# A hybrid attention layer: the widest level of the gated linear attention through a key-value state, and its prefix sums on VectorE

## The chip, the cores and the metric

The kernel runs on one core of a Trainium2 chip. The metric is the time of one execution on the device, in microseconds (us). Three runs of the kernel before took 887.92, 889.42 and 889.54 us; their median is 889.42 us. In this text PE is TensorE (the matmul engine), PEld its weight loads, DVE is VectorE, ACT is ScalarE, POOL is GpSimd, SP is SyncE, which here only issues transfers.

## The reference: what is computed

One decoder layer on a sequence of 512 tokens with 1024 channels, all in 32-bit floats: a layer norm, a token mixer of two branches, a residual layer norm, a squared-ReLU MLP of width 4096, and a last layer norm. One branch of the mixer is multi-head latent attention with 8 heads, the other gated linear attention (GLA) with 4 heads, keys of 128 channels and values of 256. This change is about the GLA branch alone. Cut to that branch, the reference is

```python
log_a = log_sigmoid(a_lr @ w_gla_a2 + b_gla_a2) / 16      # per token and key channel, <= 0
# b = cumsum(log_a) over tokens; for tokens i >= j:
# scores[i, j] = sum_d q[i, d] * k[j, d] * exp(b[i, d] - b[j, d])
# o[i] = sum_{j <= i} scores[i, j] * v[j]
o_gla = rms_norm(o) * silu(r)          # then a projection, gated and merged with the other branch
```

## The kernel before

Most matmuls take 32-bit data in a rounded format (fp32r), one record each in the trace. Each operand is split into a high part and a remainder: ACT copies the high part (`hi`), DVE subtracts it (`lo`), and each product is three matmuls, hi·hi, hi·lo and lo·hi. The helper `split` (L104 to L110) does this for activations, `pump` (L179, L180) for weights. Matmuls on plain 32-bit operands also occur; the profile shows two records for each of those.

The GLA scores are not computed in chunks but in levels. For s = 1, 2, 4, ... 256 the tokens are cut into blocks of s, and a level gives the scores between each right block (queries) and the left block beside it (keys). Each level needs the decays inside a block: `rp` holds two rows of 512 running sums, R (from a key to the end of its left block) and P (from the start of the right block to a query). `vec(s)` lets ACT take the exponential of them (E, L637) and DVE multiply keys and queries by it (M, L640 and L644). PE multiplies the halves of M to scores in a bank named `px` (L693, L696, L700). `take` copies them from the bank: DVE under a mask into the four diagonal 128x128 blocks SD for s up to 64, and by `split` for s = 128 (`s128`) and s = 256 (`s256`). `advance(s)` turns the sums of level s into those of 2s: two additions on POOL, each of 256 elements per partition (L619 for R, L620 for P). The next `vec` waits for both.

`gla_out(h)` multiplies the scores of a head with the values. With four blocks of 128 tokens there are ten pairs (j, i) with j up to i, each three matmuls with 256 columns, 30 for a head (L741 to L743). ACT squares each result with its sum (`osq`, L745), POOL and DVE normalise, DVE multiplies with the gate `Rg` (L755), PE transposes (L761).

The values V and the gates R are projected for a pair of heads at a time, in `proj_v(hp)` and `proj_r(hp)`. Each multiplies all 512 tokens with 512 weight columns, in four accumulator banks, one per block of 128 tokens. The evacuation splits each bank by head, 256 columns at a time: `Vh[h]` (two tiles, hi and lo, for all tokens of one head) and `Rg[h]`.

The order of the work comes from three things. The projections are the backbone: after each of a projection's eight inner steps, `tick` lets two "lanes" go one step, the levels (four heads in turn, `lane_levels`) and the outputs (`lane_out`). These lanes run beside proj_v(0), proj_r(0), proj_v(1), proj_r(1) and then the four gate projections "g" of the branch merge, between two of which stands the projection `qr` of the rotary queries. A guard in proj_v(1), `levels_upto(1)`, runs the levels of heads 0 and 1 to their end before that projection's banks are read out. Finally the framework simulates the program while it is built and puts each engine's instructions in the order that its simulation prefers; on the chip each engine takes its own in that fixed order and waits on semaphores. Accumulators have four banks named `mm`, all else shares four named `px`. Large tiles of 4 KB per partition come from a pool of 24 (tag A): V, R, the running sums, the split scores, and also the gate tiles `gt` of the "g" projections.

## Time and profile before

| What | Value |
|---|---|
| Median of three runs | 889.42 us |
| The profiled execution's own time | 889.34 us |
| Its span in the trace | 887.4 us |
| GLA levels and outputs in the trace | about 96 to 276 us |
| First matmul of the projection that reads the GLA output | about 322 us |
| Instructions in the trace | 11559 |

Times in the trace count from the start of the span. A row of a timeline has the start, the time of the group, engine, line, operation, what it writes and reads, the shape, and in brackets the idle time before it. A matmul's time in the trace is from its start to its modelled end, and the next one begins before that end; so the rate of PE is read from the distance between starts. Rows of groups have count, summed time and mean in ns.

### The profile page before, as it was taken

To read this page: it belongs to the slowest core of one execution; us is meant where nothing else is said; L and a number is where in the kernel's file an instruction comes from. 1 tells how busy PE (TensorE), PEld (TensorE's weight loads), DVE (VectorE), ACT (ScalarE), POOL (GpSimd) and SP (SyncE) were. 2 spreads that over 40 slices of the span, in tenths; PEclk is the share of its full clock that TensorE was granted. 3 is DMA by queue.
4 is the path that set the end of the run, shared out by engine and by line. 5 is a ranking of instruction groups with operands and counts; after the bars stand their busy time and mean duration, and the time that the engine had idled before them with its cause. 6 is when DMAs were issued, how large, how long until landed. Compare 5 with 4: busy or idle time off the path is not lost.

```text
span 887.4 us, 11559 instructions
## 1 busy us (share of the span) xinstructions
PE 866.8 (98%) x4352; PEld 738.7 (83%) x4352; DVE 573.3 (65%) x973; ACT 435.0 (49%) x740; POOL 172.5 (19%) x215
## 2 busy tenths in 40 slices
PE   5999999999999999999999999999999999999995
PEld 5988888888888888888888888988888888888884
DVE  6934875667735234557866697987557556754687
ACT  5546543445434334435654424566357546745651
POOL 2203441433511010000000013004400520241022
PEclk9999999999999999999999999999999999999998
DMA  7513223221222333111307628006941891397075
GB/s 219 159 48 95 72 72 95 72 72 50 79 80 67 94 84 101 54 42 55 118 24 262 191 71 285 1 0 167 291 113 30 254 253 33 72 312 186 1 190 95
DMA packets 63414, 101.13 MB, mean 114 GB/s; under 512 B 7777, under 2 KB 31764, under 8 KB 63360
## 3 DMA queue, kind: packets, MB, share of 16 engines
q1 hardware_dynamic: 48400, 64.04, 23.6%
q0 software_dynamic: 13040, 32.71, 15.4%
q10 hardware_dynamic: 1920, 3.66, 1.2%
q8 instruction: 34, 0.56, 0.3%
q14 instruction: 20, 0.16, 0.1%
HBM read 82.56 MB, written 3.67 MB: 97 GB/s over the span
## 4 chain that ended last, share of the span: by engine, by line
PE 90%; DVE 4%; DMA 4%; ACT 1%; issue 1%; POOL 0%; POOLq 0%; DVEq 0%; SPq 0%; ACTq 0%
PE mm L230 16%; PE mm L231 15%; PE mm L232 15%; PE mm L265 5%; PE mm L264 5%; PE mm L263 5%; PE px L1157 3%; PE px L1159 3%; PE px L1158 3%; PE mm L1157 2%; PE mm L1158 2%; PE mm L1159 2%; PE px L693 1%; DVE xl L180 1%; DMA wraw<-in_w_out_dram 1%; PE px L855 1%
## 5 line engine op out<-in xcount | busy, mean ns | idle before, releaser
L180 DVE TENSOR_TENSOR wlo<-wraw,whi 128x1024 fp32r<-128x1024 f32 (+2 forms) x102 | 117.0, 1147 | 156.1 <-ACT whi L179 149.8
L230 PE MATMUL mm<-h,whi 128*128 128x512 f32 x416 | 162.9, 393 | 0.0
L231 PE MATMUL mm<-h,whi 128*128 128x512 f32 x416 | 162.4, 390 | 0.0
L179 ACT ACTIVATE whi<-wraw 128x1024 fp32r<-128x1024 f32 (+2 forms) x102 | 99.9, 979 | 126.2 <-PE mm L231 64.9
L232 PE MATMUL mm<-h,wlo 128*128 128x512 f32 x416 | 155.7, 391 | 0.0
L1185 POOL DMA_DIRECT2D res<-ev x54 | 47.8, 988 | 238.8 <-ACT ev L1183 198.2
L232 PEld LDWEIGHTS mm<-h,wlo 128*128 128x128 f32 x416 | 78.1, 188 | 16.2
L230 PEld LDWEIGHTS mm<-h,whi 128*128 128x128 f32 x416 | 78.1, 188 | 15.7
L231 PEld LDWEIGHTS mm<-h,whi 128*128 128x128 f32 x416 | 78.1, 188 | 15.4
L264 PE MATMUL mm<-wlo,h 128*128 128x512 f32 x128 | 50.6, 395 | 0.0
L265 PE MATMUL mm<-whi,h 128*128 128x512 f32 x128 | 50.3, 394 | 0.0
L263 PE MATMUL mm<-whi,h 128*128 128x512 f32 x128 | 49.9, 400 | 0.0
L1239 ACT ACTIVATE relu<-mm 128x512 f32<-128x512 f32 x32 | 18.8, 595 | 56.7 <-PE mm L232 56.7
L354 POOL TENSOR_TENSOR mv<-mv,mhalf 128x1 f32<-128x1 f32 x4 | 4.1, 1036 | 210.5 <-DVE mv L353 210.5
L619 POOL TENSOR_TENSOR rp<-rp 128x256 f32<-128x256 f32 x32 | 30.0, 936 | 63.5 <-ACT E L637 52.8
L644 DVE TENSOR_TENSOR M<-E,qk 128x256 f32<-128x256 f32 x48 | 28.9, 628 | 12.5 <-ACT E L637 12.2
L637 ACT ACTIVATE E<-rp 128x512 f32<-128x512 f32 x32 | 20.4, 638 | 26.2 <-POOL rp L620 26.1
L179 ACT ACTIVATE xh<-wraw 128x1024 fp32r<-128x1024 f32 (+1 forms) x20 | 19.1, 962 | 27.5 <-PE mm L265 14.8
L180 DVE TENSOR_TENSOR wlo<-wq,whi 128x1024 fp32r<-128x1024 f32 x15 | 18.3, 1223 | 20.2 <-ACT whi L179 20.2
L265 PEld LDWEIGHTS mm<-whi,h 128*128 128x128 f32 x128 | 24.0, 188 | 4.9
L264 PEld LDWEIGHTS mm<-wlo,h 128*128 128x128 f32 x128 | 24.1, 188 | 4.4
L263 PEld LDWEIGHTS mm<-whi,h 128*128 128x128 f32 x128 | 24.0, 188 | 4.2
(383 smaller groups left out, 2233.8 us busy)
## 6 DMA issues: line engine op xcount, KB each, us to landing
wraw<-in_w_in_dram SPq DMA_DIRECT2D x40, 512.0 KB, 3.7
wraw<-in_w_ff_dram SPq DMA_DIRECT2D x32, 512.0 KB, 8.5
wq<-in_w_ff_dram POOLq DMA_DIRECT2D x32, 512.0 KB, 9.3
res<-ev POOLq DMA_DIRECT2D x54, 256.0 KB, 8.6
wraw<-in_w_o_gla_dram SPq DMA_DIRECT2D x8, 512.0 KB, 3.7
wraw<-in_w_o_mla_dram SPq DMA_DIRECT2D x8, 512.0 KB, 3.3
wraw<-in_w_out_dram SPq DMA_DIRECT2D x8, 512.0 KB, 4.5
wraw<-in_w_in_dram SPq DMA_DIRECT2D x8, 360.0 KB, 5.3
```

The lines of the kernel that those rows point to most:

```text
L179: st["ins"] = act(hi[:, :nk, :n], raw[:, :nk, :n], AF.Copy)
L180: vtt(lo[:, :nk, :n], raw[:, :nk, :n], f(hi[:, :nk, :n]), op=ALU.subtract)
L230: mm(o, hi[:, c], xh, start=first, stop=False)
L231: mm(o, hi[:, c], xl, start=False, stop=False)
L232: mm(o, lo[:, c], xh, start=False, stop=last)
L263: mm(o, xh, hi[:, :n], start=opens, stop=False, skip_group_check=share)
L264: mm(o, xh, lo[:, :n], start=False, stop=False, skip_group_check=share)
L265: mm(o, xl, hi[:, :n], start=False, stop=last, skip_group_check=share)
L1157: mm(o, xh[:, c], hi[:, pp, cols], start=opens, stop=False, skip_group_check=True)
L1158: mm(o, xh[:, c], lo[:, pp, cols], start=False, stop=False, skip_group_check=True)
L1159: mm(o, xl[:, c], hi[:, pp, cols], start=False, stop=hf == 1 and pp == 1, skip_group_check=True)
L1185: nc.gpsimd.dma_start(res[tt + t][:, j * T:(j + 1) * T], e, accum_op=ALU.add)
```

## The change

Four things change, all in the GLA branch.

Level 256 no longer makes scores. PE transposes the decayed keys of the first 256 tokens (two transposes of 128x128, L702 in the changed kernel, in place of two plain matmuls with 256 columns, L700). They are split into `kq[:, 0]`, the decayed queries of the last 256 tokens into `kq[:, 1]`: two splits of 256 in place of one of 512. `gla_out` then forms the state, keys times values (six matmuls, L737 to L739), splits it (`gst`, a new ACT copy and a DVE subtraction), and multiplies it with the queries of blocks 2 and 3. Per head: four diagonal products, two of level 128, two with the state and two for the state, ten of three matmuls, 30 as before.

`advance(s)` is one DVE instruction (L623) over both rows of sums, 512 elements, in place of two POOL instructions of 256.

V and the gates stay together for a pair of heads, in tiles of two token blocks (`Vp`, `Rp`): evacuations of 512 columns in place of two of 256. So the tiles of V come free when the second head of the pair has been read, and by halves of the tokens.

The guard in proj_v(1) is gone.

```diff
     def proj_v(hp, guard=None):
+        vp = []
         def e(a, j, ps):
-            for i, h in enumerate(hs):
-                if Vh[h] is None:
-                    Vh[h] = (A([P, NT, HV], F32R, "vh"), A([P, NT, HV], F32R, "vl"))
-                split(ps[:, i * HV:(i + 1) * HV], Vh[h][0][:, a, :], Vh[h][1][:, a, :])
+            if a % 2 == 0:
+                vp.append((A([P, 2, T], F32R, "vh"), A([P, 2, T], F32R, "vl")))
+            split(ps, vp[-1][0][:, a % 2, :], vp[-1][1][:, a % 2, :])
+            if a == NT - 1:
+                Vp[hp] = vp
...
     def proj_r(hp):
-                stt(Rg[h][:, a, :], th[:, i * HV:(i + 1) * HV], 1.0, ps[:, i * HV:(i + 1) * HV],
-                    op0=ALU.add, op1=ALU.mult)
+            stt(rg[-1][:, a % 2, :], th, 1.0, ps, op0=ALU.add, op1=ALU.mult)
...
         def advance(s):
-            Rv, Pv = pairs(rp[:, 0, :], s), pairs(rp[:, 1, :], s)
-            n = T // (2 * s)
-            gtt(Rv[:, :, 0, :], Rv[:, :, 0, :], Pv[:, :, 1, s - 1:s].to_broadcast([P, n, s]), op=ALU.add)
-            gtt(Pv[:, :, 1, :], Pv[:, :, 1, :], Pv[:, :, 0, s - 1:s].to_broadcast([P, n, s]), op=ALU.add)
+            v = rp[:, 0, :]
+            def view(off, side, step):
+                return bass.AP(tensor=v.tensor, offset=v.offset + off, ap=[v.ap[0], [side, 2], [2 * s, T // (2 * s)], [step, s]])
+            new = view(0, T + s, 1)
+            vtt(new, new, view(T + 2 * s - 1, -s, 0), op=ALU.add)
...
         def take(s, p):
-                s256 = A([P, 2, 2, 2 * P], F32R, "s256")
-                split(p.rearrange("p (a b) -> p a b", b=256), s256[:, 0], s256[:, 1])
+                split(p[:, :256], kq[:, 0, 0], kq[:, 0, 1])
...
                 for j in range(2):
-                    mm(p[:, j * 256:(j + 1) * 256], M[:, j * P:(j + 1) * P], M[:, 256:], start=True, stop=True)
+                    nc.tensor.transpose(p[:, j * P:(j + 1) * P], M[:, j * P:(j + 1) * P], ident)
+                kq = A([P, 2, 2, 256], F32R, "kq")
+                split(M[:, 256:], kq[:, 1, 0], kq[:, 1, 1])
...
     def gla_out(h):
+        p = PX()[:, :HV]
+        for j in range(2):
+            vh, vl = V(j)
+            kh, kl = [kq[:, 0, w, j * P:(j + 1) * P] for w in range(2)]
+            mm(p, kh, vh, start=j == 0, stop=False)
+            mm(p, kh, vl, start=False, stop=False)
+            mm(p, kl, vh, start=False, stop=j == 1)
+        sh, sl = B([P, HV], F32R, "gst"), B([P, HV], F32R, "gst")
+        split(p, sh, sl)
...
-            for j in range(i + 1):
-                mm(o, blk(j, i, 0), vh[:, j, :], start=j == 0, stop=False)
-                mm(o, blk(j, i, 0), vl[:, j, :], start=False, stop=False)
-                mm(o, blk(j, i, 1), vh[:, j, :], start=False, stop=j == i)
+            todo = [(sd[:, 0, i, :], sd[:, 1, i, :], *V(i))]
+            if i % 2:
+                todo.append((s128[:, 0, i // 2, :], s128[:, 1, i // 2, :], *V(i - 1)))
+            if i > 1:
+                c = slice((i - 2) * P, (i - 1) * P)
+                todo.append((kq[:, 1, 0, c], kq[:, 1, 1, c], sh, sl))
+            for n, (ah, al, bh, bl) in enumerate(todo):
+                mm(o, ah, bh, start=n == 0, stop=False)
+                mm(o, ah, bl, start=False, stop=False)
+                mm(o, al, bh, start=False, stop=n == len(todo) - 1)
...
-    proj_v(1, lambda: levels_upto(1))
+    proj_v(1)
```

The built programs differ as follows in counts: PE has the same number of instructions (eight plain matmuls with 256 columns become eight transposes), DVE goes from 975 to 999, ACT stays at 699, POOL goes from 220 to 156, and the transfers are the same. The order of the instructions moves in many places between the levels' first instruction and the end of the GLA outputs. Two places matter for what follows; rows are in the engine's order, names carry the buffer's number.

The first place is the passage from proj_r(1) to the first gate projection, with the levels of head 2 between them. On PE before, the last rows of the projection (L264, L265 into mm_1782), then the last level of head 2 and its transposes, then the gate projection into the bank that proj_r(1) used first:

```order
L263 MATMUL mm_1782<-whi_1912,h_33_170 128x512
L696 MATMUL px_1992<-M_1962 128x128 [waits DVE_49]
L696 MATMUL px_1992<-M_1962 128x128
L264 MATMUL mm_1782<-wlo_1913,h_33_170 128x512
L265 MATMUL mm_1782<-whi_1912,h_33_170 128x512
L700 MATMUL px_2039<-M_1998 128x256 [waits DVE_49]
L700 MATMUL px_2039<-M_1998 128x256
L711 MATMUL px_2062<-ca,SD_1705 128x128 [waits DVE_49]
L711 MATMUL px_2062<-ca,SD_1705 128x128
L230 MATMUL mm_2045<-h_12_114,whi_1976 128x512 [waits DVE_49,Activation_49]
L231 MATMUL mm_2045<-h_12_114,whi_1976 128x512
```

and on PE after the change:

```order
L263 MATMUL mm_1739<-whi_1864,h_33_170 128x512
L264 MATMUL mm_1739<-wlo_1865,h_33_170 128x512
L265 MATMUL mm_1739<-whi_1864,h_33_170 128x512
L695 MATMUL px_1943<-M_1913 128x128 [waits DVE_49]
L695 MATMUL px_1943<-M_1913 128x128
L695 MATMUL px_1988<-M_1949 128x128 [waits DVE_49,PE_49]
L695 MATMUL px_1988<-M_1949 128x128
L230 MATMUL mm_1997<-h_12_114,whi_1927 128x512 [waits DVE_49]
L231 MATMUL mm_1997<-h_12_114,whi_1927 128x512
```

Level 256 has moved behind this place, and level-64 and level-32 matmuls (L695) stand in the gap. On DVE before, `ogT` is the normalised output of head 1, L601 (`rg`) reads the banks of proj_r(1), mm_1770 first:

```order
L640 TENSOR_TENSOR M_1998<-E_1996,qk_748 128x512 [waits Activation_49]
L110 SCALAR_TENSOR_TENSOR ogT_1966<-px_1939,cb,ogT_1966 128x512 [waits Activation_49]
L653 COPY_PREDICATED SD_1705<-cmask,px_1956 128x2x2x64 [waits DVE_49,PE_49]
L601 SCALAR_TENSOR_TENSOR rg_2017<-th_2015,mm_1770 128x256 [waits Activation_49]
L601 SCALAR_TENSOR_TENSOR rg_2019<-th_2015,mm_1770 128x256
L110 SCALAR_TENSOR_TENSOR ogT_2000<-px_1969,cb,ogT_2000 128x512 [waits Activation_49]
L601 SCALAR_TENSOR_TENSOR rg_2017<-th_2021,mm_1774 128x256 [waits Activation_49]
L601 SCALAR_TENSOR_TENSOR rg_2019<-th_2021,mm_1774 128x256
```

and on DVE after, where mm_1727 is the first of those banks:

```order
L656 COPY_PREDICATED SD_1746<-cmask,px_1907 128x2x8x16 [waits DVE_49,PE_49]
L110 SCALAR_TENSOR_TENSOR ogT_1917<-px_1890,cb,ogT_1917 128x512 [waits Activation_49]
L647 TENSOR_TENSOR M_1949<-E_1947,qk_748 128x2x2x64 [waits Activation_49]
L647 TENSOR_TENSOR M_1949<-E_1947,qk_748 128x2x2x64
L623 TENSOR_TENSOR rp_1743<-rp_1743 128x2x4x64
L110 SCALAR_TENSOR_TENSOR ogT_1953<-px_1920,cb,ogT_1953 128x512 [waits Activation_49]
L601 SCALAR_TENSOR_TENSOR rg_1970<-th_1968,mm_1727 128x512 [waits Activation_49]
L601 SCALAR_TENSOR_TENSOR rg_1970<-th_1972,mm_1731 128x512 [waits Activation_49]
```

The new advance (L623) and both `ogT` rows now stand ahead of the first L601, whose bank the first gate matmul (L230) waits for.

The second place is the output of head 3, the last, and the projection `qr` behind it (L263, reading latT). On PE before, the end of head 3 and the first matmuls of `qr`:

```order
L741 MATMUL px_2497<-vh_1720,s_471_2418 128x256
L742 MATMUL px_2497<-vl_1721,s_471_2418 128x256
L743 MATMUL px_2497<-vh_1720,s_471_2418 128x256
L741 MATMUL px_2497<-vh_1720,sd_2441 128x256
L742 MATMUL px_2497<-vl_1721,sd_2441 128x256
L743 MATMUL px_2497<-vh_1720,sd_2441 128x256
L263 MATMUL mm_2549<-whi_2481,latT_831 128x256 [waits Activation_49]
L264 MATMUL mm_2549<-wlo_2482,latT_831 128x256 [waits DVE_49]
```

and after, where L739 in the rows ahead of these has closed the state, gst_2482 is its high part and gst_2483 its remainder:

```order
L756 MATMUL px_2515<-vl_1694,sd_2439 128x256
L757 MATMUL px_2515<-vh_1693,sd_2439 128x256 [waits DVE_49]
L755 MATMUL px_2515<-gst_2482,kq_2415 128x256 [waits Activation_49]
L755 MATMUL px_2487<-vh_1681,sd_2439 128x256 [waits Activation_49]
L756 MATMUL px_2487<-vl_1682,sd_2439 128x256
L757 MATMUL px_2487<-vh_1681,sd_2439 128x256
L755 MATMUL px_2487<-vh_1681,s_484_2418 128x256
L756 MATMUL px_2487<-vl_1682,s_484_2418 128x256
L757 MATMUL px_2487<-vh_1681,s_484_2418 128x256
L756 MATMUL px_2515<-gst_2483,kq_2415 128x256 [waits DVE_49]
L757 MATMUL px_2515<-gst_2482,kq_2415 128x256
L263 MATMUL mm_2501<-whi_2423,latT_831 128x256 [waits Activation_49]
```

On ACT before, where L945 (`gt`) reads the four banks of the gate projection:

```order
L745 ACTIVATE osq_2469,gss_2464<-px_2465 128x256 [waits PE_49]
L745 ACTIVATE osq_2477,gss_2464<-px_2465 128x256 [waits PE_49]
L745 ACTIVATE osq_2507,gss_2464<-px_2497 128x256
L945 ACTIVATE gt_2521<-mm_2325,hbg 128x512 [waits PE_49]
L945 ACTIVATE gt_2523<-mm_2326,hbg 128x512 [waits PE_49]
L945 ACTIVATE gt_2531<-mm_2327,hbg 128x512 [waits PE_49]
L179 ACTIVATE whi_2527<-wraw_2479 128x1024 [waits DMAHW0_49,DVE_49,PE_49]
L945 ACTIVATE gt_2533<-mm_2328,hbg 128x512 [waits DVE_49,PE_49]
```

and after, where that line is L960:

```order
L106 ACTIVATE gst_2482<-px_2475 128x256 [waits PE_49]
L759 ACTIVATE osq_2491,gss_2486<-px_2487 128x256
L960 ACTIVATE gt_2459<-mm_2259,hbg 128x512 [waits PE_49]
L960 ACTIVATE gt_2461<-mm_2260,hbg 128x512 [waits PE_49]
L759 ACTIVATE osq_2499,gss_2486<-px_2487 128x256
L759 ACTIVATE osq_2522,gss_2486<-px_2515 128x256 [waits PE_49]
L960 ACTIVATE gt_2469<-mm_2261,hbg 128x512 [waits DVE_49,PE_49,Pool_49]
L960 ACTIVATE gt_2471<-mm_2262,hbg 128x512 [waits PE_49]
```

In the changed kernel the tile gt_2459 takes the buffer of vl_1682, gt_2461 that of vh_1681, gt_2469 that of sd_2439 and gt_2471 that of vl_1694, all of which head 3 still reads; before, three of the four took buffers of the R tile of head 2, of head 3's running sums and of its queries and keys, which head 3's output doesn't read, and only the fourth that of s_477_2447, which it does. In the built program the first gate evacuation waits for the matmul L756 that reads vl_1682 with s_484_2418, and the first matmul of `qr` waits for that evacuation, whose bank it takes.

More of the change, by code (lines that the diff above doesn't have):

```diff
@@ L597, in e @@
             act(th, ps, AF.Tanh, scale=0.5)
-            for i, h in enumerate(hs):
-                if Rg[h] is None:
-                    Rg[h] = A([P, NT, HV], F32, "rg")
-                stt(Rg[h][:, a, :], th[:, i * HV:(i + 1) * HV], 1.0, ps[:, i * HV:(i + 1) * HV],
-                    op0=ALU.add, op1=ALU.mult)
+            if a % 2 == 0:
+                rg.append(A([P, 2, T], F32, "rg"))
+            stt(rg[-1][:, a % 2, :], th, 1.0, ps, op0=ALU.add, op1=ALU.mult)
+            if a == NT - 1:
+                Rp[hp] = rg
         gemm_tm([PL["r", hp]], hT, T, e)
@@ L649, in take @@
         def take(s, p):
-            nonlocal s128, s256
+            nonlocal s128, kq
             if s <= 64:
@@ L717, in gla_levels, with V @@
         split(pt, sd[:, 0, 2:], sd[:, 1, 2:])
-        SS[h] = (sd, s128, s256)
+        SS[h] = (sd, s128, kq)
         yield
     def gla_out(h):
-        while SS[h] is None or Vh[h] is None or Rg[h] is None:
+        while SS[h] is None or Vp[h // 2] is None or Rp[h // 2] is None:
             yield
-        sd, s128, s256 = SS[h]
-        def blk(j, i, w):
-            if i == j:
-                return sd[:, w, i, :]
-            if j // 2 == i // 2:
-                return s128[:, w, j // 2, :]
-            return s256[:, w, j, (i - 2) * P:(i - 1) * P]
-        vh, vl = Vh[h]
+        sd, s128, kq = SS[h]
+        def V(j):
+            c = slice(h % 2 * HV, (h % 2 + 1) * HV)
+            return [t[:, j % 2, c] for t in Vp[h // 2][j // 2]]
+        p = PX()[:, :HV]
[7 more added lines that the diff above has]
+        split(p, sh, sl)
         ss = S([P, NT], F32, "gss")
```

12 lines of the change are left out of this document (6 added, 6 removed).

## The prediction

> **What bounds the kernel now.** I read the page's busy times first, then what PE waited for, then the stretches in which the GLA branch runs.
>
> ```profile
> PE 866.8 (98%) x4352; PEld 738.7 (83%) x4352; DVE 573.3 (65%) x973; ACT 435.0 (49%) x740; POOL 172.5 (19%) x215
> ```
>
> A busy PE alone would prove little, since matmul ends are modelled. The list of waits for PE settles it; its columns are total us, times and longest:
>
> ```profile
> PE px L369 <- ACT x L358: 8.5, 1, 8.5
> PE mm L265 <- POOL h L377: 0.5, 1, 0.5
> PE mm L264 <- DVE xl L180: 0.4, 1, 0.4
> PE px L369 <- DVE x L360: 0.4, 1, 0.4
> PE mm L230 <- ACT h L372: 0.3, 1, 0.3
> ```
>
> That is all of it, and it stands on the lines of layer norms and of the first weights. While GLA runs, PE waits for nobody. So the time falls by exactly the PE work that goes, and rises by each wait that PE gets; faster POOL, DVE or ACT work by itself is worth nothing. Busy time by stretch (window, length, then PE, PEld, DVE, ACT, POOL) shows where an engine could come to be late:
>
> ```profile
> 105.00:130.00 25.00, 25.00 (x133) 21.34 (x132) 22.73 (x42) 13.53 (x28) 14.12 (x18) 1.00 0.29 85
> 155.00:180.00 25.00, 24.95 (x141) 21.66 (x140) 17.75 (x32) 13.60 (x30) 9.83 (x13) 1.00 0.22 64
> 205.00:230.00 25.00, 25.00 (x135) 21.60 (x134) 15.92 (x32) 11.87 (x27) 8.11 (x10) 1.00 0.29 85
> ```
>
> DVE is at 22.7 of 25 us in the levels of head 0, with less than 18 in the later ones.
>
> **Level 256 on PE.** Starts in the timeline give the price of the old products and of a pair of transposes like the new ones:
>
> ```profile
> 251.99 1.02 PE L700 MATMUL px<-M 128*128 128x256 f32 x4
> 252.66 0.58 PE L230 MATMUL mm<-h,whi 128*128 128x512 f32 x1
> 253.08 0.40 PE L231 MATMUL mm<-h,whi 128*128 128x512 f32 x1
> 253.32 0.40 PE L232 MATMUL mm<-h,wlo 128*128 128x512 f32 x1
> ...
> 255.62 0.38 PE L711 MATMUL px<-ca,SD 128*128 128x128 f32 x2
> 255.76 0.48 PE L230 MATMUL mm<-h,whi 128*128 128x512 f32 x1
> 256.08 0.40 PE L231 MATMUL mm<-h,whi 128*128 128x512 f32 x1
> 256.31 0.40 PE L232 MATMUL mm<-h,wlo 128*128 128x512 f32 x1
> ```
>
> From the first L700 to L231 are 1.09 us, one 512-column matmul among them; the next such step is 0.24, about 0.23 elsewhere (256.08 to 256.31). So the four records cost 1.09 - 0.23 = 0.86 us. The two transposes: 0.46 - 0.23 = 0.23 us. A head saves 0.63 us, four heads 2.5 us. The 30 matmuls of the outputs stay 30, with the same 256 columns, so I take nothing for them.
>
> **What else moves, and its cover.** The profile's groups from 95 to 280 us, and the spread of the products M:
>
> ```profile
> L644 DVE TENSOR_TENSOR M<-E,qk 128x256 f32<-128x256 f32 x48 | 28.9, 628 | 12.5 <-ACT E L637 12.2
> L107 DVE TENSOR_TENSOR vl<-mm,vh 128x256 fp32r<-128x256 f32 x16 | 6.0, 412 | 0.1
> L619 POOL TENSOR_TENSOR rp<-rp 128x256 f32<-128x256 f32 x32 | 30.0, 936 | 63.5 <-ACT E L637 52.8 <-DVE rp L611 10.8
> L620 POOL TENSOR_TENSOR rp<-rp 128x256 f32<-128x256 f32 x32 | 24.0, 750 | 9.7 <-ACT q L663 7.5
> ...
> L644 DVE TENSOR_TENSOR M<-E,qk x48: 408/518/957, 101.9 to 242.2; 128x256 f32<-128x256 f32 x48
> ...
> L640 DVE TENSOR_TENSOR M<-E,qk x8: 676/692/1109, 118.2 to 245.6; 128x512 f32<-128x512 f32 x8
> ```
>
> The trace has no advance on DVE. Its nearest row is L640: two inputs and an output in SBUF, 512 elements. Free of POOL it takes 0.69 us, the largest is 1.11, and half the size costs 0.41; I take 0.69 and keep 0.41 and 1.11 as ends. The 32 advances put 32 x 0.69 = 22 us on DVE, and 54 us leave POOL. The products M had the additions on POOL beside them (32 x (0.94 + 0.75) us). Their lowest is 0.41, their mean 0.63, so with POOL out of the way they should give back up to 48 x 0.22 = 10 us of DVE time. On the way from level to level two POOL additions of 1.69 us become one step of 0.69: the levels run ahead rather than late. Evacuations of V and gates halve in number, 0.69 against 2 x 0.41; the extra splits (kq, `gst`) give it back. All of this lies beside PE and costs nothing as long as DVE keeps up.
>
> The Trainium skill bears on the M rows: the page "SBUF — State Buffer", section "Who interferes with whom", says that a DVE instruction with two SBUF inputs and a POOL instruction that reads SBUF exclude each other, and the second to come waits for the first to end. The trace agrees with the 957 ns maximum against 408. By that rule all 48 products fall to 0.41 us and DVE's net load rises by some 12 us over the stage; if the slowness had another cause it would rise by 22, the first stretch would not hold, and the time would be that of the DVE rival below.
>
> Does it hold? In 105 to 130 us stand 12 of the 48 products, two L640, and eight new advances. DVE instructions that wait for nothing overlap by some 0.1 us (below, one starts at 208.72, before the end of the last at 208.38 + 0.45 = 208.83), so an advance occupies 0.6. Advances: 8 x 0.6 = 4.8. Products: -12 x 0.22 = -2.6; one L640 back from 1.11: -0.4. V: four at 0.69 for eight at 0.41, -0.5. So 22.7 + 1.3 = 24.0 of 25 us. It holds, with 1.0 us to spare, that is for advances of up to 0.81 us.
>
> **The new waits.** First place, from proj_r(1) to the gate projection. Before, DVE and PE met like this:
>
> ```profile
> 208.38 0.45 DVE L653 COPY_PREDICATED SD<-cmask,px 128x256 f32<-128x256 uint8 x1
> 208.72 0.73 DVE L601 SCALAR_TENSOR_TENSOR rg<-th,mm 128x256 f32<-128x256 f32 x2
> ...
> 209.07 1.03 PE L700 MATMUL px<-M 128*128 128x256 f32 x4
> 209.93 0.38 PE L711 MATMUL px<-ca,SD 128*128 128x128 f32 x2
> 210.07 0.49 PE L230 MATMUL mm<-h,whi 128*128 128x512 f32 x1
> ```
>
> The bank was free at 209.45, PE came at 210.07: 0.62 us to spare, because L700 and L711 (1.0 us) lay between. After, four L695 rows lie there, two records each, about 0.9 us, so 0.1 less; and an advance of 0.69 stands ahead of the evacuation. 0.62 - 0.1 - 0.69 = -0.2, plus the step of a semaphore: I put down a wait of 0.3 us. Its ends are none, and 1.4: the three DVE rows behind the last M (0.69 + 0.74 + 0.69, less overlap, 1.9) less the half of the gap's matmuls that this M releases (0.45).
>
> Second place, the end of head 3:
>
> ```profile
> 267.60 0.28 PE L743 MATMUL px<-vh,sd 128*128 128x256 f32 x1
> 267.72 0.28 PE L263 MATMUL mm<-whi,latT 128*128 128x256 f32 x1
> ...
> 264.31 0.38 ACT L745 ACTIVATE osq<-px 128x256 f32<-128x256 f32 x1
> 264.66 0.69 ACT L945 ACTIVATE gt<-mm,hbg 128x512 f32<-128x512 f32 x1
> ```
>
> Before, gates were read at 264.66 to 265.4, `qr` began at 267.72: 2.4 us of cover. After, it goes thus, from the start of the state's last matmul. It ends at 0.28, its copy on ACT (priced as the square, 0.38) at 0.66. PE has four matmuls of 0.12 to do, till 0.48: a wait of 0.2. The square behind the copy ends at about 0.95, PE is there at 0.78: 0.2 more. The fifth matmul from there (vl_1682 with s_484_2418) starts at 1.43 and ends at 1.71; the gate takes 0.69, to 2.40. PE has finished its eight matmuls at 1.91: 0.5. Together 0.9 us. The copy's and the square's waits could vanish if PE arrives late; the gate's 0.69 against 0.36 us of cover can't. I keep 0.4 and 1.5 as ends.
>
> **The sum.** -2.5 + 0.3 + 0.9 = -1.3 us, against the profiled execution's own 889.34 us (span 887.4, 1.9 around it): 888.0. The median of the runs, 889.42, lies 0.1 above that execution. Everything after the GLA stage has the same instructions and stays PE's, so the shift passes to the end.
>
> **Rivals.** *The waits don't come.* If PE reaches both places later, or DVE runs ahead, since the levels lose 1 us per level of POOL time, the 2.5 us stay but for the gate's 0.4: 887.2; without any, 886.8. For it: PE waited nowhere in this stage before, with DVE at 22.7 of 25. Against: the order has taken the cover away at both places.
>
> *DVE becomes the bound.* The advance is a strided operation in place, one input a broadcast; if it takes over 0.81 us, the first stretch is full, and the remainders of weights (L180), which PE needs, queue behind the levels. At the upper end of 1.11: 8 x 0.42 = 3.4 less the 1.0 to spare, 2.4 us of wait there, and the first place goes from 0.3 to its 1.4: 888.0 + 2.4 + 1.1 = 891.5, slower. For it: L640 and L644 did reach 1.11 and 0.96. Against: only with POOL beside them, which falls silent.
>
> *The gain is eaten.* Waits at their upper ends, 1.4 + 1.5, with the advance as priced: 889.7, no change.
>
> **How the numbers follow.** A measurement of this kernel can tell about 0.2%, 1.8 us, from no change; the three runs spread over 1.6 us. The forecast, 887.6 to 889.0, has 0.42; the gain eaten 0.10: both within 0.2%. The waits not coming, 886.6 to 887.6, has 0.33, nearly all of it faster by over 0.2%. DVE as the bound, 890.6 to 893, has 0.15, of it 0.13 slower by over 0.2%. So faster 0.33, same 0.54, slower 0.13. The range leaves out the worse half of the DVE case: 886.4 to 890.8. The forecast's own range is 887.6 to 889.0.
>
> **What would show it.** The new transposes (L702) as two records some 0.11 us apart, with no L700. The advance (L623) near 0.69 us; M (L647) near 0.42 throughout. In PE's waits: the gate's L230 on DVE `rg`, about 0.3 us once; L755 and L263 at head 3 on ACT, about 0.9 us together; else none. The first matmul of the projection that reads the GLA output 1.3 us earlier than at 322. I'm wrong if PE shows waits on DVE in the first V or R projection, or if the 256-column products with the state take other than 0.12 us a step.

## The result: 1.2 us faster, near the sum, in which errors cancel

| | before | changed |
|---|---|---|
| Median, same chip, 22 runs each | 888.68 us | 887.45 us |
| Ratio, 95% interval | | 0.9985, 0.9979 to 0.9991 |
| The profiled execution's own time | 889.34 us | 887.92 us |
| Its span | 887.4 us | 885.9 us |
| First matmul that reads the GLA output | 322.5 us | 321.2 us |

The change is worth 0.15%, less than the 0.2% that a measurement was said to tell from no change; with 22 runs on each side the interval lies below 1 all the same. The forecast, 888.0 us, was set against the profiled execution, which went from 889.34 to 887.92. The median, 887.45, lies just under the forecast's own range of 887.6 to 889.0, because the kernel before came out at 888.68 over 22 runs and not at the 889.42 of its first three; the medians differ by 1.2 us where 1.3 was forecast. The shift at the first matmul after the stage is 1.3 us, and PE reaches the last transposes ahead of the stage (L496) at 81.6 us in both traces, so all of it was made in the stretch that the prediction spoke of.

The page of the changed kernel, engines first:

```profile
PE 863.9 (98%) x4344; PEld 735.7 (83%) x4344; DVE 578.6 (65%) x997; ACT 437.0 (49%) x740; POOL 118.2 (13%) x151
```

PE is 2.9 us less busy, DVE hardly more (573.3 before), POOL 54 us less. What PE waited for (total us, times, longest):

```profile
PE mm L263 <- ACT gt L960: 0.4, 1, 0.4
...
PE mm L230 <- DVE rg L601: 0.3, 1, 0.3
```

Both rows are new, and are the two places of the prediction; the other rows are those of before, on layer norms and first weights, 10.1 us in all before and 10.7 now. The new and the changed operations, by line (nanoseconds lowest/median/largest, then first and last start in us):

```profile
L702 PE MATMUL px<-ca,M x8: 270/271/273, 124.4 to 257.9; 128*128 128x128 f32 x8
...
L623 DVE TENSOR_TENSOR rp<-rp x32: 676/684/693, 100.5 to 251.2; 128x512 f32<-128x512 f32 x32
...
L647 DVE TENSOR_TENSOR M<-E,qk x48: 402/420/468, 102.0 to 247.9; 128x256 f32<-128x256 f32 x48
```

The advance takes 0.684 us (0.69 was priced), the 48 products M are at 0.42, the largest at 0.47 (it was 0.96), and the transposes L702 are eight records in the place of 16 of L700. Busy time by stretch (length, PE, PEld, DVE, ACT, POOL):

```profile
105.00:130.00 25.00, 25.00 (x134) 21.28 (x133) 21.78 (x46) 13.06 (x24) 0.74 (x1) 1.00 0.29 85
```

In the levels of head 0 DVE is at 21.8 of 25 us, not at the 24.0 of the forecast.

The first place, DVE and then PE in the timeline of the changed kernel:

```profile
205.47 0.68 DVE L623 TENSOR_TENSOR rp<-rp 128x512 f32<-128x512 f32 x1
206.07 0.74 DVE L110 SCALAR_TENSOR_TENSOR ogT<-px,cb,ogT 128x512 fp32r<-128x512 f32 x1
206.73 1.27 DVE L601 SCALAR_TENSOR_TENSOR rg<-th,mm 128x512 f32<-128x512 f32 x2
...
206.14 1.05 PE L695 MATMUL px<-M 128*128 128x128 f32 x8
207.46 0.50 PE L230 MATMUL mm<-h,whi 128*128 128x512 f32 x1 [0.27 <-DVE rg L601]
```

The eight records of L695 begin at 206.14 and follow each other every 0.11 us; the gate's matmul could have begun at about 207.0. It waits 0.44 us by the starts (the bracket counts 0.27, from the modelled end). Ahead of the evacuation stand the advance and a row of `ogT`, each about as long as the evacuation itself. The second place, the end of head 3:

```profile
262.95 0.28 PE L757 MATMUL px<-vh,sd 128*128 128x256 f32 x1
263.35 0.38 PE L755 MATMUL px<-gst,kq 128*128 128x256 f32 x1
263.71 0.39 PE L755 MATMUL px<-vh,sd 128*128 128x256 f32 x1
...
264.65 0.28 PE L757 MATMUL px<-gst,kq 128*128 128x256 f32 x1
265.35 0.39 PE L263 MATMUL mm<-whi,latT 128*128 128x256 f32 x1 [0.42 <-ACT gt L960]
```

Steps here are 0.12 us. The distances 262.95 to 263.35, 263.35 to 263.71 and 264.65 to 265.35 are longer by 0.28, 0.25 and 0.59: the state's copy, the square, the gate, 1.1 us together, where 0.2 + 0.2 + 0.5 had been put down.

### The profile page after: what moved, and what is told of

The parts are those of the page before. It is cut to its first block, busy times and chain, and to the rows that moved or that the text cites. A ratio compares the mean times of both kernels' runs of the same rounds, so it can differ in the third digit from the quotient of the medians.

```text
span 885.9 us, 11482 instructions
## 1 busy us (share of the span) xinstructions
PE 863.9 (98%) x4344; PEld 735.7 (83%) x4344; DVE 578.6 (65%) x997; ACT 437.0 (49%) x740; POOL 118.2 (13%) x151
## 4 chain that ended last, share of the span: by engine, by line
PE 95%; DMA 2%; DVE 1%; issue 0%; ACT 0%; POOLq 0%; DVEq 0%; SPq 0%; POOL 0%; ACTq 0%
PE mm L230 16%; PE mm L231 16%; PE mm L232 16%; PE mm L265 6%; PE mm L264 6%; PE mm L263 6%; PE px L1172 3%; PE px L1173 3%; PE px L1174 3%; PE mm L1173 2%; PE mm L1174 2%; PE mm L1172 2%; PE px L695 1%; PE px L870 1%; PE px L265 1%; PE px L264 1%
## 5 line engine op out<-in xcount | busy, mean ns | idle before, releaser
L180 DVE TENSOR_TENSOR wlo<-wraw,whi 128x1024 fp32r<-128x1024 f32 (+2 forms) x102 | 116.2, 1139 | 142.7 <-ACT whi L179 136.4
L230 PE MATMUL mm<-h,whi 128*128 128x512 f32 x416 | 162.1, 391 | 0.3 <-DVE rg L601 0.3
L230 PEld LDWEIGHTS mm<-h,whi 128*128 128x128 f32 x416 | 78.2, 188 | 16.4 <-DVE rg L601 0.5
L264 PE MATMUL mm<-wlo,h 128*128 128x512 f32 x128 | 50.9, 398 | 0.0
L265 PE MATMUL mm<-whi,h 128*128 128x512 f32 x128 | 50.2, 393 | 0.0
L263 PE MATMUL mm<-whi,h 128*128 128x512 f32 x128 | 49.5, 399 | 0.0
L180 DVE TENSOR_TENSOR wlo<-wq,whi 128x1024 fp32r<-128x1024 f32 x15 | 18.3, 1223 | 20.4 <-ACT whi L179 20.4
L265 PEld LDWEIGHTS mm<-whi,h 128*128 128x128 f32 x128 | 24.1, 188 | 4.7
L263 PEld LDWEIGHTS mm<-whi,h 128*128 128x128 f32 x128 | 24.0, 188 | 4.2
L264 PEld LDWEIGHTS mm<-wlo,h 128*128 128x128 f32 x128 | 24.1, 188 | 4.0
L230 PE MATMUL mm<-ogT,whi 128*128 128x512 f32 x64 | 25.7, 401 | 0.0
L1115 POOL DMA_DIRECT2D wq<-in_w_ff_dram x32 | 24.0, 921 | 10.3 <-PE mm L264 5.8
```

The lines of the kernel that those rows point to most:

```text
L180: vtt(lo[:, :nk, :n], raw[:, :nk, :n], f(hi[:, :nk, :n]), op=ALU.subtract)
L230: mm(o, hi[:, c], xh, start=first, stop=False)
L263: mm(o, xh, hi[:, :n], start=opens, stop=False, skip_group_check=share)
L264: mm(o, xh, lo[:, :n], start=False, stop=False, skip_group_check=share)
L265: mm(o, xl, hi[:, :n], start=False, stop=last, skip_group_check=share)
```

## The experiments

| Kernel | Median, us | Ratio to before (95%) | First matmul that reads the GLA output, us |
|---|---|---|---|
| State, guard away | 887.57 | 0.9987 (0.9979 to 0.9996) | 321.3 |
| Advance alone | 888.38 | 1.0000 (0.9991 to 1.0009) | 322.7 |
| Guard away alone | 888.26 | 0.9995 (0.9986 to 1.0004) | 322.2 |
| Pairs, guard away | 890.99 | 1.0029 (1.0018 to 1.0041) | 324.8 |
| State, guard kept | 893.32 | 1.0049 (1.0036 to 1.0062) | 327.1 |
| Changed, guard put back | 895.65 | 1.0079 (1.0065 to 1.0092) | 329.4 |
| Changed, advance on POOL | 887.94 | 0.9996 (0.9988 to 1.0005) | 322.0 |
| Changed, one more yield | 886.72 | 0.9974 (0.9964 to 0.9984) | 320.9 |
| Changed, `kq` from the other pool | 887.10 | 0.9976 (0.9966 to 0.9986) | 320.8 |
| Changed, both, and `sd` | 885.62 | 0.9963 (0.9951 to 0.9975) | 319.3 |
| Changed, advance and 512 more | 897.75 | 1.0106 (1.0090 to 1.0122) | 330.3 |
| Changed, advance and 128 more | 896.18 | 1.0081 (1.0067 to 1.0094) | 330.6 |

The kernel before ran beside each (888.6 to 889.0). Since the framework orders the instructions anew for each program, every edit here is the edit and the order that comes with it. The last column is from one trace each, and part of its differences arises ahead of the stage: PE reaches L496 at 81.6 us in the traces of before and of the change, at 81.1 to 82.1 in the others. Where this matters below, the stage's own length is given, from L496 to that first matmul.

### The parts alone

**The state**, in the kernel before, with V and gates by head and the advance on POOL; the guard is away too.

```diff
-                    mm(p[:, j * 256:(j + 1) * 256], M[:, j * P:(j + 1) * P], M[:, 256:], start=True, stop=True)
+                    nc.tensor.transpose(p[:, j * P:(j + 1) * P], M[:, j * P:(j + 1) * P], ident)
+                kq = A([P, 2, 2, 256], F32R, "kq")
+                split(M[:, 256:], kq[:, 1, 0], kq[:, 1, 1])
...
-    proj_v(1, lambda: levels_upto(1))
+    proj_v(1)
```

> The kernel before with the key-value state of level 256 and without the guard in proj_v(1); V and gates stay per head, the advance stays on POOL. Theory (the gain is the PE work of level 256): 2.5 us less PE work, with waits only where V's or the state's copies come late; since V per head frees other buffers than V per pair, the waits at the end of head 3 need not be the same, and I expect 0.5 to 1.5 us of waits in all: 1.0 to 2.0 us faster than before. Rival (the gain comes from the advance on VectorE, which shortens the chain from level to level): no faster than before.

It came out 1.2 us faster, all of the change's gain. PE has waits that before has not, at the outputs of head 0:

```profile
PE px L751 <- ACT sd L106: 0.7, 1, 0.7
...
PE mm L263 <- DVE vl L107: 0.3, 1, 0.3
```

By the starts they are 0.90 and 0.44 us, about what is missing of 2.5 in the medians. In the trace, where PE reaches L496 0.4 us later than in before, the stage itself is 1.7 us shorter. So the gain is the PE work of level 256, less whatever wait the new order happens to make.

**The advance** on DVE, in the kernel before.

```diff
-            gtt(Rv[:, :, 0, :], Rv[:, :, 0, :], Pv[:, :, 1, s - 1:s].to_broadcast([P, n, s]), op=ALU.add)
-            gtt(Pv[:, :, 1, :], Pv[:, :, 1, :], Pv[:, :, 0, s - 1:s].to_broadcast([P, n, s]), op=ALU.add)
+            new = view(0, T + s, 1)
+            vtt(new, new, view(T + 2 * s - 1, -s, 0), op=ALU.add)
```

> The kernel before with the advance as one VectorE instruction, nothing else. Theory: PE's work is unchanged and PE had no wait to lose, so the time stays within 0.5 us of before; the advances take 0.69 us, the products M fall from a mean of 0.63 to 0.42 us since POOL is silent. Rival (the shorter chain from level to level is the gain): 1 us or more faster. Rival (VectorE becomes the bound): 2 us or more slower.

No change: 22 us of advances more on DVE (5 us net, 578.5 against 573.3 us busy, as the products M are faster), 54 us less on POOL, and neither is seen in the time.

**The guard** away, in the kernel before.

```diff
-    proj_v(1, lambda: levels_upto(1))
+    proj_v(1)
```

> The kernel before with that line alone taken away. Theory (in before PE waits for nobody in this stage, so an order that only loosens this binding moves nothing): no change, within 0.5 us of before, ratio 0.9995 to 1.0005, first matmul that reads the GLA output at 322.2 to 322.8. Rival (the line itself costs or saves): a wait of PE in 95 to 320 us that before has not, or small steps that go, 0.5 us or more either way.

No change that the interval could tell (-0.05%), and no new wait.

**V and gates per pair**, in the kernel before, the guard away as above.

```diff
+            if a % 2 == 0:
+                vp.append((A([P, 2, T], F32R, "vh"), A([P, 2, T], F32R, "vl")))
+            split(ps, vp[-1][0][:, a % 2, :], vp[-1][1][:, a % 2, :])
...
+            stt(rg[-1][:, a % 2, :], th, 1.0, ps, op0=ALU.add, op1=ALU.mult)
```

> The kernel before with values and gates per head pair, and the line taken away; level 256 and the advance as before. Theory (half as many evacuations at 0.69 us for two of 0.41 lie beside PE): no change, within 0.5 us of before. Rival (the buffers of a pair are held until its second head is done, so the next to use them come later): a wait of PE on the lines that use these pools, up to about 1 us, near the outputs of head 3 (262 to 270 us).

2.4 us slower: the theory fails, and the rival has one of two places, without its cause. PE's waits:

```profile
PE mm L230 <- DVE rg L601: 1.2, 1, 1.2
PE px L745 <- ACT osq L749: 0.9, 1, 0.9
```

The second lies near 267 us, where the rival expected one. But PE waits there for a `px` bank that ACT is still squaring, not for a buffer that a pair of heads holds. The first is at the prediction's first place. There DVE has this ahead of the evacuation:

```profile
206.00 1.19 DVE L645 TENSOR_TENSOR M<-E,qk 128x256 f32<-128x256 f32 x2
207.11 0.44 DVE L654 COPY_PREDICATED SD<-cmask,px 128x256 f32<-128x256 uint8 x1
207.45 1.39 DVE L110 SCALAR_TENSOR_TENSOR ogT<-px,cb,ogT 128x512 fp32r<-128x512 f32 x2
208.76 1.86 DVE L601 SCALAR_TENSOR_TENSOR rg<-th,mm 128x512 f32<-128x512 f32 x3
```

Two rows of `ogT` and products M of 0.6 us each, with POOL's additions beside them. The four parts alone do not add up to the change: -1.2 (the state, with the guard away), 0, -0.3 (the guard, within its interval) and +2.4 (the pairs, with the guard away).

### The guard with the state

The state once more, and the whole change once more, both with the guard's line kept.

```diff
-    proj_v(1)
+    proj_v(1, lambda: levels_upto(1))
```

> The same as the run before it, with the guard kept: the levels of heads 0 and 1 are run to their end before the banks of proj_v(1) are read out. If the guard is neutral, as it looks in the kernel before, where PE waits for nobody: the same time as without it. If the levels' last steps then stand between the projections with nothing beside them, each costs part of its chain (ACT 0.64, VectorE 0.42 to 0.84 twice, POOL 1.69 us): waits of 2 to 4 us on VectorE, and the kernel is slower than without the guard by that much, so 0 to 3 us slower than before.

> The changed kernel with the one line put back that made proj_v(1) wait in the order until the levels of head 1 stand ahead of it. In the first study of the state with this line and the advance on POOL, PE waited 2.8 and 0.4 us on DVE M near 209 to 212, ran at about half its pace for some 5 us after that, and the kernel was 4.4 us slower than before. Theory (the line binds PE to the levels' latency from step to step, and the two output passes that cover it are not at hand there): PE waits on M there again, though less, since a level takes one DVE row of 0.69 us where it took 1.69 us of POOL: 1 to 3 us slower than the changed kernel, 888.5 to 890.5, ratio to before 1.000 to 1.002. Rival (with the advance on DVE the levels are early enough): no wait on M, within 0.5 us of the changed kernel.

Both expectations miss in size, the second by far: with the guard the state is 5.8 us slower (893.32 against 887.57, with 2.8 us the longest wait, on M as expected), and the changed kernel 8.2 us. In the latter PE's row of work between proj_r(1) and the gate projection is this:

```profile
205.03 1.05 PE L695 MATMUL px<-M 128*128 128x128 f32 x8
206.40 1.11 PE L776 MATMUL px<-ca,og 128*128 128x128 f32 x4 [0.32 <-DVE og L769]
209.31 0.71 PE L695 MATMUL px<-M 128*128 128x128 f32 x4 [1.80 <-DVE M L647]
...
211.93 1.20 PE L698 MATMUL px<-M 128*128 128x128 f32 x4 [1.47 <-DVE M L643]
213.92 0.66 PE L702 MATMUL px<-ca,M 128*128 128x128 f32 x2 [0.80 <-DVE M L643]
...
214.66 0.78 PE L230 MATMUL mm<-h,whi 128*128 128x512 f32 x1
```

With the guard the last levels of head 2 stand in PE's order bare, one behind the other, and no projection's matmul lies between them; PE goes at the pace of exponential, product and advance, and of what else DVE has in its order between these: ahead of the M that ends the wait of 1.80 stand the gated rows `og` (1.65 us) and a weight remainder (1.22). Before had L700 and L711 there as well, but its projection's last rows still stood among them. And around these waits PE's granted clock falls, to 0.66 in 210 to 215 us and 0.50 in 215 to 218 (last section), which makes some 2 us of the loss. So the guard's line, which costs nothing that the interval shows in the kernel before, costs 8 us in the changed one, and its removal is a part that the change could not do without.

### The change with the advance back on POOL

```diff
-            vtt(new, new, view(T + 2 * s - 1, -s, 0), op=ALU.add)
+            gtt(Rv[:, :, 0, :], Rv[:, :, 0, :], Pv[:, :, 1, s - 1:s].to_broadcast([P, n, s]), op=ALU.add)
+            gtt(Pv[:, :, 1, :], Pv[:, :, 1, :], Pv[:, :, 0, s - 1:s].to_broadcast([P, n, s]), op=ALU.add)
```

> The changed kernel with the advance put back on POOL, nothing else. Theory: the wait for the gate's bank behind proj_r(1), 0.44 us in the changed kernel, goes, since no advance stands ahead of the evacuation any more; the waits at the end of head 3 stay; so 0.2 to 0.6 us faster than the changed kernel, about 886.9 us, and the products M are back at a mean near 0.63 us with maxima of 0.9. Rival (the advance on VectorE is worth something by itself): slower than the changed kernel by 0.5 us or more.

A miss, in the sign: the wait at the first place should have gone, and grew. The median is 0.5 us above that of the changed kernel, just where the rival begins.

```profile
PE mm L230 <- DVE rg L601: 0.6, 1, 0.6
```

The products M are slow again:

```profile
L645 DVE TENSOR_TENSOR M<-E,qk x48: 407/657/964, 102.4 to 249.1; 128x256 f32<-128x256 f32 x48
```

At the first place two of them take 1.19 us instead of 0.75, and in the new order more stands behind them, ahead of the evacuation:

```profile
206.04 0.45 DVE L654 COPY_PREDICATED SD<-cmask,px 128x256 f32<-128x256 uint8 x1
206.38 1.39 DVE L110 SCALAR_TENSOR_TENSOR ogT<-px,cb,ogT 128x512 fp32r<-128x512 f32 x2
```

A masked copy and both rows of `ogT` replace the advance of 0.68 and one row of `ogT`. What the advance on DVE pays in the changed kernel is not settled. The ratios, 0.9996 and 0.9985, have intervals that overlap; the first matmul that reads the GLA output comes 0.7 us later (321.99 against 321.25), but PE reached L496 0.5 us later, so the stage itself is only 0.2 us longer.

### The three waits

The evacuation moved ahead of the rows of `ogT`, by a further yield in the outputs:

```diff
-            if i >= 1:
-                yield
+            yield
```

> The changed kernel, but the generator of the outputs gives way once more, after the first block of a head too. That moves the evacuation into rg at the first place ahead of both gated rows of the head before on DVE, and puts transposes of og beside the four L695 rows on PE. Theory (a wait is a matter of what stands ahead of the evacuation on its engine): the wait of L230 on DVE rg, 0.44 us by the starts, goes to none; the waits at the end of head 3 (0.28, 0.25 and 0.59 us) stay within 0.3 us. So 0.4 us less than the changed kernel: about 887.0, ratio to before 0.998. Rival (DVE is late in that stretch as a whole): the wait stays, or moves to the next row that reads DVE, and the time is that of the changed kernel.

`kq` from the pool of smaller tiles, which orders the end of head 3 anew:

```diff
-                kq = A([P, 2, 2, 256], F32R, "kq")
+                kq = [B([P, 2, 256], F32R, "kq") for _ in range(2)]
```

> The changed kernel with kq as two tiles of 2 KB from the other pool of buffers, which changes what the scheduler puts beside the end of head 3. Theory (the 1.1 us there come from the state's copy, the square and the gate following each other on ACT with nothing between on PE): the waits on the copy and the square go (0.28 + 0.25), the gate's 0.59 stays or shrinks to 0.5; the wait at the first place, 0.44, stays. About 0.5 us less than the changed kernel: 886.9 to 887.0. Rival (the 512 elements of state splitting per head cost ACT or DVE time wherever they stand): the sum of the waits at head 3 stays near 1.1 us, and the time is that of the changed kernel.

Both, and `sd` in two tiles of that pool:

```diff
-        sd = A([P, 2, NT, P], F32R, "sd")
+        sd = [B([P, 2, 2, P], F32R, "sd") for _ in range(2)]
```

> Both edits together, and sd too as two tiles of the other pool. Theory (all that the change lost of its 2.5 us is three waits at two places): no wait of PE in the whole GLA stage, so the full 2.5 us stand: 889.34 - 2.5 = 886.8 on the scale of the profiled execution, some 886.2 beside a median of 888.7 for the kernel before; ratio 0.9972, faster than the changed kernel by 1.2 to 1.5 us. First matmul that reads the GLA output near 320.0 (322.5 before, 321.25 with the change). Rival (the products with the state, or the way PE's steps run, cost some of the 2.5 us): the waits go but the time stays within 0.4 us of the changed kernel.

The yield takes the wait at the first place away. In its timeline a row of transposes of `og` (L775) and one of L695 lie ahead of the gate's L230, which follows at its usual step; the first `rg` on DVE starts at 204.56 and takes 0.69 us, so it is done in time:

```profile
206.37 0.60 PE L775 MATMUL px<-ca,og 128*128 128x128 f32 x4
206.81 0.61 PE L695 MATMUL px<-M 128*128 128x128 f32 x4
207.17 0.48 PE L230 MATMUL mm<-h,whi 128*128 128x512 f32 x1
```

At head 3 0.26 (the square) and 0.42 (the gate) stay, the copy's wait goes too. With `kq` from the other pool it is the other way round: the first place keeps its 0.44, the copy and the square go, the gate keeps 0.59. All three edits together leave PE no wait in the stage, by the matmuls as here and by the weight loads:

```profile
PE px L369 <- ACT x L358: 8.7, 1, 8.7
PE mm L265 <- POOL h L377: 1.3, 1, 1.3
PE px L369 <- DVE x L360: 0.5, 1, 0.5
PE mm L230 <- ACT h L372: 0.3, 1, 0.3
```

This kernel has the lowest median, 885.62 us, 3.3 below before, with an interval that does not touch that of the changed kernel, though it overlaps those of the two edits by themselves. Its trace shows the same at the first reader of the GLA output:

```profile
L230 PE MATMUL mm<-ogT,whi x64: 387/389/481, 319.3 to 384.4; 128*128 128x512 f32 x64
```

3.2 us earlier than before, of which 0.2 were there at L496, so the stage is 3.0 shorter where 2.5 was expected. Adding up the distances from each start to the next by the line of the first, in the traces of before and of this kernel: level 256 went from 3.07 to 0.54 us for the four heads (-2.53), the outputs from 14.79 to 14.85, the two transposes of SD from 0.84 to 0.54, and the other products of the levels from 15.54 to 15.01. The 0.3 at SD is no cheaper transpose but a wait, for a distance counts the wait of the row that follows. In the kernel before, the first product of a head's levels (L677) starts at 178.08, 0.32 us after the second transpose, where 0.07 is the usual step. The view counts a wait from a matmul's modelled end and passes this one by; among the weight loads of before it stands:

```profile
PEld px L677 <- ACT vh L106: 0.3, 1, 0.3
```

So PE did wait once in this stage before, by 0.3 us, and the order of this kernel has no such wait. The rest, some 0.2 us, is in small pieces among the levels and stays open.

### More load on DVE

Behind each advance one more addition on DVE into a tile that nothing reads, first of 512, then of 128 elements:

```diff
             vtt(new, new, view(T + 2 * s - 1, -s, 0), op=ALU.add)
+            vtt(B([P, T], F32, "dup"), rp[:, 0, :], rp[:, 1, :], op=ALU.add)
```

> The changed kernel with a second addition of 512 elements behind each advance, into a tile that nothing reads: the output is the same, DVE alone has 32 more rows of about 0.69 us, 0.6 us each with overlap, 19 us in all. In the first stretch (105 to 130 us) DVE stood at 21.8 of 25 us with the change; eight more of 0.6 make 26.6. The prediction's rival (DVE as the bound, from an advance of 0.81 us on): PE waits on DVE there by at least 1.6 us, and at the first place by 0.6 us more: 889.7 or later, 2 us slower than the changed kernel. If DVE has more room than its busy share shows (its work can slip to the next stretch, 13 of 25 us busy): PE waits for less than 0.5 us more in all, and the time stays within 0.7 us of the changed kernel.

> The changed kernel with a second addition behind each advance as in the run before, but of 128 elements: the nearest row of that size, x from q and qk, takes 0.32 us, 0.2 with overlap, so 32 x 0.2 = 6.4 us more on DVE, a third of the run before. In the first stretch DVE had 3.2 of 25 us to spare with the change (21.8 busy), and 8 x 0.2 = 1.6 stays within that. Theory with a threshold (the wait begins when a stretch is full): only the places that wait anyway grow, the first one by at most 0.4: within 0.6 us of the changed kernel. Rival (each added microsecond of DVE counts in proportion, from the first on): a third of 9 us, some 3 us slower than the changed kernel, 890.5.

They were meant to find the load at which DVE becomes the bound, and they did not. The larger load costs 10.3 us by the medians, well beyond the 2 of its rival, and the smaller one 8.7, where its theory had 0.6 at most and its rival 3. The added rows are 32 times 0.686 and 0.285 us:

```profile
L624 DVE TENSOR_TENSOR dup<-rp x32: 676/686/698, 99.8 to 264.0; 128x512 f32<-128x512 f32 x32
```

```profile
L624 DVE TENSOR_TENSOR dup<-rp x32: 276/285/321, 100.4 to 262.2; 128x128 f32<-128x128 f32 x32
```

That is 22.0 against 9.1 us of added work, and PE comes out of the stage 9.1 and 9.4 us later than in the changed kernel: the loss does not follow the load. (The traces are closer than the medians since PE's clock fell once in the first and twice in the second.) In both the first stretch (105 to 130 us) has no wait of PE at all, though the larger one brings DVE to 23.82 of 25 us; the waits stand at the outputs of head 0, at the first place and at head 3. The run with the small addition:

```profile
PE mm L230 <- DVE rg L601: 2.5, 1, 2.5
PE px L756 <- DVE ogT L110: 1.5, 1, 1.5
...
PE px L738 <- ACT kq L106: 0.8, 1, 0.8
```

DVE's order at the first place shows how a row of 0.28 us can go with a wait of 2.5 there:

```profile
209.95 0.74 DVE L110 SCALAR_TENSOR_TENSOR ogT<-px,cb,ogT 128x512 fp32r<-128x512 f32 x1
210.61 0.28 DVE L624 TENSOR_TENSOR dup<-rp 128x128 f32<-128x128 f32 x1
210.81 0.43 DVE L657 COPY_PREDICATED SD<-cmask,px 128x256 f32<-128x256 uint8 x1
211.30 1.23 DVE L180 TENSOR_TENSOR wlo<-wraw,whi 128x1024 fp32r<-128x1024 f32 x1
212.44 0.43 DVE L657 COPY_PREDICATED SD<-cmask,px 128x256 f32<-128x256 uint8 x1
212.77 1.87 DVE L601 SCALAR_TENSOR_TENSOR rg<-th,mm 128x512 f32<-128x512 f32 x3
```

A weight remainder (L180) and two masked copies have come to stand between `ogT` and `rg`, where the changed kernel has nothing. The scratch tile takes its turn in the pool of smaller tiles, and the order of all engines moved; whether the pool or the added row itself moved it was not separated. Where a load with the order unchanged would begin to hurt was not tried and stays open.

## Why the prediction was right, step by step

**PE's saving.** -2.5 us were forecast for level 256. By distances of starts, its rows went from 3.07 to 0.70 us in the changed kernel, -2.4, and to 0.54, -2.5, in the kernel without waits. Right. That the outputs' 30 matmuls cost what they did is right too (14.85 against 14.79 without waits).

**The first place** was put at 0.3 and measured 0.44. The mechanism is the one described, the evacuation that comes late behind an advance; the yield that moves it forward removes the wait. The size came from the old order's spare 0.62 us. In the new one the last M ends at 205.55; behind it advance, `ogT` and evacuation last until 207.41, the 1.9 us that the prediction used for its upper end, and PE is done with the products of the gap at 207.02. That gives the 0.4 directly.

**The second place** was put at 0.9 and measured 1.1, each of its three parts 0.05 to 0.1 larger than priced. Both places together are 0.35 us worse than the sum had them.

**What made up for that** was not forecast. "While GLA runs, PE waits for nobody" was read from a view that passes short waits by: the kernel before had the one of 0.3 us at L677, and the changed order does without it. With it the account closes: -2.5 + 0.4 + 1.1 - 0.3 = -1.3, the stage's measured shift. The run with the guard alone away lacks this wait too, and its stage is 0.4 us shorter. So the three terms of the sum are right in kind, but that their total is right to a tenth is luck: the 0.35 us that the two places cost more and the 0.3 us of old wait that went cancel.

**The advance and M.** 0.69 priced, 0.684 measured; M from a mean of 0.63 to 0.42. The Trainium skill's rule that the prediction leaned on (page "SBUF — State Buffer", section "Who interferes with whom") agrees with these traces: with POOL silent the largest M is 0.47 us, with the advance back on POOL 0.96. The trace of before shows it row by row: 22 of the 48 products take 0.41 to 0.46 us; each of the other 26 began while a POOL instruction was running, and ended 0.28 us after that one did. The mean of 0.63 is this mixture.

**DVE's first stretch**: 24.0 of 25 us forecast, 21.8 measured. The products gave 3.1 us back instead of 2.6, and a weight remainder of 1.2 us moved out of the stretch. The rival that makes DVE the bound therefore had less behind it than its 0.15. Its place is doubtful too: in the runs with added load a stretch at 23.82 of 25 us made no wait there, and the waits came later, at the outputs and at the gate, though in an order that had moved.

**Two steps that fail outside the whole.** "All of this lies beside PE and costs nothing" was said of V and gates per pair, among others: alone they cost 2.4 us, at the very two places. What covers this in the change is not shown. It is not the fast M: with the advance back on POOL, M at a mean of 0.65 us and the pairs kept, the median is still 0.8 us below before (the interval reaches 1), not 2.4 above. The order that comes with the state is left as the candidate. And the guard's removal was costed at nothing without a word: true in the kernel before within the interval, but with the state in, the guard costs 5.8 to 8.2 us. The time of the whole was right since the waits were read from the changed kernel's own order, not from the parts.

## What to carry to other kernels

Where PE hardly waits, work taken from PE is worth its distance of starts; here 2.5 us were expected and, once no wait was left, the stage was 3.0 shorter. Ask the weight loads too before you say that PE waits for nobody. Everything else in such an edit was paid here at a few places, where one projection's banks pass to the next and where a head's output waits for its copies, and there by what stands ahead on DVE or ACT. Read these places in the changed order and price them; a part of an edit that is free alone may be ruinous or necessary beside another. And look there for the next gain: one yield and another pool for two tiles gave more (1.8 us by the medians) than the whole change had (1.2).

## What the runs showed of the hardware

**PE's clock was halved for a while after a wait of only 1.5 us.** In the run with the small addition, PE starts nothing from 177.81 to 179.58 where a step is 0.12 us, and goes on so:

```profile
179.58 0.36 PE L756 MATMUL px<-vh,sd 128*128 128x256 f32 x1 [1.49 <-DVE ogT L110]
...
180.78 0.63 PE L265 MATMUL mm<-whi,h 128*128 128x512 f32 x1
...
183.34 0.63 PE L265 MATMUL mm<-whi,h 128*128 128x512 f32 x1
...
184.54 0.39 PE L263 MATMUL mm<-whi,h 128*128 128x512 f32 x1
```

The step is 0.43 us where it is 0.23 otherwise, about eight steps long, so the wait of 1.5 is followed by a loss of some 1.6 more. The granted clock in a window of the same trace (third number from the end) agrees:

```profile
182.00:184.00 2.00, 2.00 (x6) 1.55 (x5) 0.82 (x2) 0.00 (x0) 0.00 (x0) 0.52 0.00 0
```

In the run of the pairs a wait of 1.2 us had no such effect (1.00 in every window of 2 us behind it); with the 2.8 us wait of the state with the guard the clock was at 0.50 from 212 to 217. What a fall costs shows in that kernel's five runs too: the one with a mean granted clock of 0.997 took 890.63 us, the four at 0.992 to 0.994 took 893.21 to 893.66. The Trainium skill (page "TensorE: Matmul & The Clock Gate", section "HAM oscillation — how this bites in real kernels") gives about 3.4 us as the length of a gap to avoid. These traces disagree: less than half of that was enough once, and the measurement decides. Where between 1.2 and 1.5 us it begins, or whether more than the length of the gap counts, these runs do not show.

**A DVE row of two inputs from SBUF** took 0.285 us with 128 elements and 0.686 with 512: about 0.15 us and 1.04 ns for each element, on which the products M lie too (0.42 with 256). The estimate for the small one had been 0.32; the row it was taken from, x, has a median of 0.28 in the trace of the change.
